# Scaling the input on VectorE instead of GpSimd, with four constants and one DMA rule of the build-time order changed

## The chip, the cores and the metric

The kernel runs on one core of one Trainium2 chip. The metric is the device time of one execution in microseconds; for the kernel before, three timed runs gave 2083.99, 2084.95 and 2100.44 us, with a median of 2084.95 us. In profile rows PE is TensorE (PEld its weight loads), DVE is VectorE, ACT is ScalarE, POOL is GpSimd and SP is SyncE, which issues most DMAs.

## The reference: what is computed

One decoder layer is applied to 256 prompt tokens and to 8 x 8 sample tokens with the same weights. All arrays are float32.

```python
def decoder_layer(x, st, p):
    hn = rmsnorm(x, p['norm1'])                 # x * rsqrt(mean(x^2) + 1e-6) * g
    proj = hn @ p['w_in']                       # 2048 -> 12752 columns
    ...
    y_s5 = s5_mixer(...)                        # diagonal state space
    y_rw = rwkv7_mixer(...)                     # 64-wide matrix state per head
    y_gd = gdn_mixer(...)                       # gated delta rule in chunks of 64,
                                                # with a triangular solve per chunk
    merged = (sigmoid(gt_s5) * (y_s5 @ p['w_br_s5']) + sigmoid(gt_rw) * (y_rw @ p['w_br_rwkv'])
              + sigmoid(gt_gd) * (y_gd @ p['w_br_gdn']))
    x = x + merged @ p['w_out']
    up = rmsnorm(x, p['norm2']) @ p['ffn_w_up']
    ...                                         # depthwise convolution, bias, gate
    return x + (silu(gate) * val) @ p['ffn_w_down'], new_states
```

A final rmsnorm follows. Outputs are the activations of all 320 tokens and the new states.

## The kernel before, in words

**Layout.** Channels lie on the 128 partitions and the 320 tokens on the free axis. Every large product multiplies a 128x128 block of weights by a [128, 320] slice of activations. To keep float32 accuracy with the fast float32r format, both sides are split into a high and a low part (`split`, line 399: ScalarE copies the high part, VectorE subtracts it to get the low part), and `products` (line 573) issues three matmuls per block: high-high, high-low and low-high. These are the wide products; there are 12720 of them, 24 to a step, and a step is one 512 KB weight tile of eight blocks.

**Weights.** `run_steps` (line 568) goes through 530 steps in a fixed order: the S5 input columns, the other columns of `w_in`, the branch products, `w_out`, `w_up` and `w_down`. `load_to` (line 426) fetches a tile into one of four `wraw` buffers with a DMA on SP; the load of step n + 4 is issued when the split of step n is done. ScalarE writes `whi` and VectorE `wlo` in halves of 128x512, into one of three pairs of buffers, so a tile can be split at the earliest when the step three before it has been multiplied.

**Between the wide products.** The recurrent branches are Python generators (`Task`), which are advanced between the blocks of the wide stream by `poll` (line 550). What they issue on TensorE are small products, many of them with tiles of fewer than 128 rows or columns.

**What sets the order.** The order of all instructions on all engines is fixed while the program is built. `Clock` (lines 112 to 225) keeps an estimated time per engine; `issue` (line 182) adds the estimated cost of each instruction, and a DMA's estimated landing time (lines 184 to 201) tells when a task that waits for it may go on. `able` (line 540) decides whether a task may be advanced now: what it reads must be ready, the engines that its next piece uses must not be estimated further than `LEAD` ahead of TensorE, and a piece with small products needs enough `heat`, a credit that wide products build up (lines 218 to 222; `PACE` and `HEAT` on line 115) and small products spend. `BURST` (line 333) is how much estimated time one call of `poll` may add to TensorE, `START` (line 334) the least credit with which a switch from wide to small products may begin, and the 0.0 at the end of line 544 the loss that is assumed of a piece that has not been issued before.

**Places that the change touches.** `norm1` (lines 630 to 661) computes the first rmsnorm. While the S5 columns and the next four columns are multiplied with an input that is not yet normalised (`xg`, made by `prep`, line 625), it gathers the squares, gets `rstd` and then, for each of the 16 channel tiles k, lets GpSimd multiply `x[:, k]` by `rstd` in place (line 658) and, one tile behind, calls `scaled` (line 403): ScalarE writes `high` with the gain `g1` as its scale, VectorE writes `low` as x times gain minus high. From step 16 plus 8 on, the wide products read `high` and `low`; `in_step` (line 678) waits for `norm1` there.

`tri_inverse` (line 1166) inverts the unit triangular matrices of the gated delta rule, 80 of them: four stores write them to the DRAM tile `gdn`, a load brings them back as `triw` with one matrix on each of 80 partitions (rows of 4096 bytes), VectorE eliminates in 60 small tensor_tensor instructions (two for each m from 1 to 30, lines 1190 to 1196), and two more stores and six loads bring the result back. It is used a second time for the rwkv branch.

Of the kernel before, what the change touches and what calls it, by code (L numbers as in the profile page):

```python
# [13 lines left out]
OP = mybir.AluOpType  # L14
# [97 lines left out]
class Clock:  # L112


    PACE, HEAT = 1.15, 800
    LAT = {"pe": 197, "dve": 127, "act": 143, "pool": 120, "dma": 1100}
    TO_SMALL, TO_WIDE, FORM = 90, 160, 140

# [63 lines left out]
    def issue(self, eng, name, outs, ins, a, k):  # L182
        t = self.begin(eng, outs, ins)
        if name == "dma_start":
            n = int(np.prod(outs[0].shape)) * 4
            row = min(run(outs[0]), run(ins[0])) * 4
            cost = n / 360.0 * (1 if row >= 512 else 3)
            if eng == "pool":
                self.t[eng] = t + 1040
                self.later.append((t + 1850, cost))  # L190
                end = max(self.dma, t + 1850) + cost
            else:
                q = self.queue = self.t[eng] = max(self.queue, t + 25) + 450
                while self.later and self.later[0][0] < q + 650:
                    at, c = self.later.pop(0)
                    self.dma = max(self.dma, at) + c
                end = self.dma = max(self.dma, q + 650) + cost
            if row < 4096:
                end += 300 if row >= 2560 else 900
            self.done("dma", outs, ins, end)  # L200
            return t, end + self.LAT["dma"]
        cost = COST[eng](name, outs, ins, a, k)
        if eng == "pe":
            wide = ins[0].dtype == F32R
            form = None if wide else (name, ins[0].shape[0], free_size(ins[0]), outs[0].shape[0])
            if form != self.form:
                t = max(t, self.t[eng] + (self.TO_WIDE if wide else self.FORM if self.form else self.TO_SMALL))
            self.form = form
            lo, n = self.box(outs[0])[1][0] % 128, outs[0].shape[0]
            cols = set(range(lo // 32, (lo + n + 31) // 32))  # L210
            if name == "matmul" and not wide and t == self.t["pe"] and self.cols and not cols & self.cols:
                cost = 0.85 * n
                self.cols |= cols
            else:
                self.cols = cols if name == "matmul" and not wide else None
        end = t + cost
        if eng == "pe":
            used = free_size(outs[0]) * (1 if wide else 4) * ins[0].shape[0] / 128
            if name == "matmul":
                used *= free_size(ins[0]) / 128  # L220
            self.lost = max(self.lost - used + self.PACE * (end - t), 0.0)
            self.heat = min(self.HEAT, self.heat + used - self.PACE * (end - self.t[eng]))
        self.t[eng] = end
        self.done(eng, outs, ins, end)
        return t, self.after("", eng, end)


def run(ap):

    n = 1  # L230
    for s, c in reversed(ap.ap[ap.space != "DRAM":]):
        if s != n and c > 1:
            break
        n *= c
    return n


def free_size(ap):
    return int(np.prod(ap.shape[1:]))
# [90 lines left out]
class Kernel:  # L330
    LEAD = 2100
    SLACK = -300
    BURST = 1500
    START = 600
    IDLE = 300
    PARTS = 2
    MARGIN = 1
# [202 lines left out]
    def able(self, t):  # L540
        now = self.now()
        if t.over or t.busy or t.ready > now + self.SLACK or t.need and len(self.spare) <= t.need or t.cond and not t.cond():
            return False
        uses, lost = self.uses.get(t.place(), (("pe", "dve", "act"), 0.0))
        c = self.clock
        if "pe" in uses and c.heat < (lost if c.form else max(lost, self.START)) and now == c.t["pe"]:
            return False
        return all(e == "pe" or self.clock.t[e] <= now + self.LEAD * (1 if t.rank else 2) for e in uses)

    def poll(self):  # L550

        end = self.clock.t["pe"] + self.BURST
        c = self.clock.t
# [76 lines left out]
    def norm1(self):  # L630

        nc, x = self.nc, self.x
        sums = self.mid.tile([128, 3, 2, T], F32, tag="hh", name="squares")
        acc, *sqs = (sums[:, j] for j in range(3))
        for i in range(KD // 2):
            pair = x[:, 2 * i:2 * i + 2]
            self.wait(pair)
            yield
            sq = sqs[i % 2] if i else acc
            nc.scalar.activation(sq, pair, AF.Square)  # L640
            yield
            if i:
                nc.vector.tensor_tensor(acc, acc, sq, op=OP.add)
        nc.vector.tensor_tensor(acc[:, 0], acc[:, 0], acc[:, 1], op=OP.add)
        yield 1
        p = self.bank()
        nc.tensor.matmul(p, self.mean, acc[:, 0], start=True, stop=True)
        yield
        r = self.st.tile([128, T], F32, tag="gt0", name="rstd")
        self.rstd_of(p, r, acc[:, 1])  # L650
        self.free(p)
        self.rs1 = r
        yield
        yield lambda: self.prepared >= KD // 2
        self.hn = self.halves()
        for k in range(KD + 1):
            if k < KD:
                nc.gpsimd.tensor_tensor(x[:, k], x[:, k], r, op=OP.mult)
            if k:
                self.scaled(x[:, k - 1], self.V("g1", k - 1), *self.hn[k - 1])  # L660
            yield 0

    def first_step(self, i):
# [1568 lines left out]
```

## Time and profile before

| | |
|---|---|
| timed runs | 2083.99, 2084.95, 2100.44 us |
| the profiled execution's own time | 2083.18 us |
| its span, first to last instruction | 2081.3 us |
| mean granted TensorE clock | 0.997 |
| PE busy, matmuls | 2049.8 us, 14557 |
| DVE busy | 1355.7 us |
| ACT busy | 1009.6 us |
| POOL busy | 249.1 us |
| 1000 to 1050 us: matmuls in 50 us | 343 |

The profile lists for each engine when an instruction began, how long it took, and, in square brackets, how long the engine had idled before it and which engine's or DMA's work ended that idle time. All rows name line 298, because a helper records every instruction; the tiles' names tell them apart. A matmul's duration includes its passage through the array, so two matmuls overlap in the rows; what counts is how many begin in a stretch. The time that lies outside the span is 2083.18 - 2081.3 = 1.9 us.

### The profile page before, as it was taken

Reading aid. Unit: us, or ns where it says so; the run is one execution under the profiler, and the core shown is the slowest. Engines: PE = TensorE matmul, PEld = TensorE weight load, DVE = VectorE, ACT = ScalarE, POOL = GpSimd, SP = SyncE. Lnnn points to the kernel's source line nnn. Section 1 sums busy time; section 2 is a strip of 40 time slices with the busy share of each in tenths; the row PEclk is TensorE's granted clock in tenths of the full one; section 3 lists DMA queues with packets and bytes.
Section 4 is the critical chain, followed back from the end, with each engine's and each line's share of the span. In section 5 each row is a group of like instructions: output and inputs, shape, how many; then the busy total and the mean of one; then the engine's idle time right before and its main releaser. Section 6 shows DMA issues by size and latency. Waiting matters only on the chain.

```text
span 2081.3 us, 37242 instructions
## 1 busy us (share of the span) xinstructions
PE 2049.8 (98%) x14557; PEld 1997.6 (96%) x14557; DVE 1355.7 (65%) x2535; ACT 1009.6 (49%) x1911; POOL 249.1 (12%) x467
## 2 busy tenths in 40 slices
PE   8999999999999999999999999999999999999997
PEld 8899999999899999889999999999999999999997
DVE  7989999776267676166855666666544466666444
ACT  6666666643245854343444444444333344444442
POOL 1312102100000000000000222222100022222000
PEclk9999999999999999999999999999999999999999
DMA  7575565556447546357755544544444444444552
GB/s 241 196 245 152 165 194 179 185 173 193 153 166 259 185 153 181 102 179 218 221 178 165 153 151 153 151 147 150 152 152 149 147 151 152 152 146 150 167 153 101
DMA packets 132353, 351.71 MB, mean 169 GB/s; under 512 B 27040, under 2 KB 53712, under 8 KB 131920
## 3 DMA queue, kind: packets, MB, share of 16 engines
q1 hardware_dynamic: 131280, 346.21, 53.0%
q0 software_dynamic: 752, 3.10, 0.4%
q8 instruction: 114, 1.87, 0.4%
q14 instruction: 63, 0.52, 0.1%
q10 hardware_dynamic: 144, 0.01, 0.0%
HBM read 320.20 MB, written 29.06 MB: 168 GB/s over the span
## 4 chain that ended last, share of the span: by engine, by line
PE 58%; DVE 0%; ACT 0%; DVEq 0%; issue 0%; ACTq 0%
PE bank L298 58%; DVE xf L298 0%; DVE acc L298 0%; ACT rstd L298 0%; DVE rstd L298 0%; DVE x L298 0%; ACT sq L298 0%; DVEq L2228 0%; ACTq L298 0%
## 5 line engine op out<-in xcount | busy, mean ns | idle before, releaser
L298 ACT ACTIVATE whi<-wraw 128x512 fp32r<-128x512 f32 x1060 | 614.7, 625 | 672.1 <-issue 376.5
L298 DVE TENSOR_TENSOR wlo<-wraw,whi 128x512 fp32r<-128x512 f32 x1060 | 699.7, 695 | 358.8 <-ACT whi L298 349.7
L298 PE MATMUL bank<-high,whi 128*128 128x320 f32 x1728 | 546.5, 316 | 0.0
L298 PE MATMUL bank<-high,wlo 128*128 128x320 f32 x1728 | 532.6, 308 | 3.4 <-DVE wlo L298 3.4
L298 PE MATMUL bank<-low,whi 128*128 128x320 f32 x1728 | 532.4, 308 | 0.0
L298 PE MATMUL bank<-x2h,whi 128*128 128x320 f32 x1408 | 435.3, 309 | 0.0
L298 PE MATMUL bank<-x2l,whi 128*128 128x320 f32 x1408 | 435.1, 309 | 0.0
L298 PE MATMUL bank<-x2h,wlo 128*128 128x320 f32 x1408 | 435.1, 309 | 0.0
L298 PEld LDWEIGHTS bank<-high,whi 128*128 128x128 f32 x1728 | 324.6, 188 | 14.3 <-issue 9.7
L298 PEld LDWEIGHTS bank<-high,wlo 128*128 128x128 f32 x1728 | 324.5, 188 | 3.9 <-DVE wlo L298 3.9
L298 PEld LDWEIGHTS bank<-low,whi 128*128 128x128 f32 x1728 | 324.9, 188 | 2.0
L298 PEld LDWEIGHTS bank<-x2l,whi 128*128 128x128 f32 x1408 | 264.3, 188 | 0.1
L298 PEld LDWEIGHTS bank<-x2h,whi 128*128 128x128 f32 x1408 | 264.3, 188 | 0.1
L298 PEld LDWEIGHTS bank<-x2h,wlo 128*128 128x128 f32 x1408 | 264.3, 188 | 0.0
L298 PE MATMUL bank<-hidl,whi 128*128 128x320 f32 x704 | 216.5, 308 | 0.0
L298 PE MATMUL bank<-hidh,wlo 128*128 128x320 f32 x704 | 216.5, 307 | 0.0
L298 PE MATMUL bank<-hidh,whi 128*128 128x320 f32 x704 | 216.5, 307 | 0.0
L298 POOL COPY blk<-blk 128x62 f32<-128x62 f32 x88 | 63.7, 724 | 627.6 <-DVE blk L298 627.6
L298 PEld LDWEIGHTS bank<-hidh,whi 128*128 128x128 f32 x704 | 131.9, 187 | 0.0
L298 PEld LDWEIGHTS bank<-hidh,wlo 128*128 128x128 f32 x704 | 131.9, 187 | 0.0
L298 PEld LDWEIGHTS bank<-hidl,whi 128*128 128x128 f32 x704 | 131.9, 187 | 0.0
L298 DVE TENSOR_TENSOR blk<-bank,rstd 128x320 f32<-128x320 f32 x88 | 43.3, 492 | 127.5 <-PE bank L298 127.5
(337 smaller groups left out, 2168.1 us busy)
## 6 DMA issues: line engine op xcount, KB each, us to landing
wraw<-w_in SPq DMA_DIRECT2D x192, 512.0 KB, 3.8
wraw<-w_up SPq DMA_DIRECT2D x176, 512.0 KB, 3.5
wraw<-w_down SPq DMA_DIRECT2D x80, 512.0 KB, 3.5
wraw<-w_out SPq DMA_DIRECT2D x32, 512.0 KB, 3.5
shs<-gst SPq DMA_DIRECT2D x16, 512.0 KB, 3.8
wraw<-w_br_g SPq DMA_DIRECT2D x16, 512.0 KB, 4.6
gates<-ev SPq DMA_DIRECT2D x48, 160.0 KB, 2.4
gt<-gates SPq DMA_DIRECT2D x48, 160.0 KB, 3.6
```

Source lines behind the costliest of these rows:

```text
L298: return f(*a, **k)
```

## The change

```diff
@@ -112,7 +112,7 @@ class Clock:
-    PACE, HEAT = 1.15, 800
+    PACE, HEAT = 1.2, 1000
@@ -197,6 +197,8 @@ def issue, for a dma_start
                 end = self.dma = max(self.dma, q + 650) + cost
             if row < 4096:
                 end += 300 if row >= 2560 else 900
+            elif outs[0].shape[0] < 128:
+                end += 1500
             self.done("dma", outs, ins, end)
@@ -330,8 +332,8 @@ class Kernel:
-    BURST = 1500
-    START = 600
+    BURST = 2000
+    START = 800
@@ -541,7 +543,7 @@ def able
-        uses, lost = self.uses.get(t.place(), (("pe", "dve", "act"), 0.0))
+        uses, lost = self.uses.get(t.place(), (("pe", "dve", "act"), 600))
@@ -655,9 +657,9 @@ def norm1
         for k in range(KD + 1):
             if k < KD:
-                nc.gpsimd.tensor_tensor(x[:, k], x[:, k], r, op=OP.mult)
+                nc.vector.scalar_tensor_tensor(out=x[:, k], in0=x[:, k], scalar=self.V("g1", k), in1=r, op0=OP.mult, op1=OP.mult)
             if k:
-                self.scaled(x[:, k - 1], self.V("g1", k - 1), *self.hn[k - 1])
+                self.split(x[:, k - 1], *self.hn[k - 1])
             yield 0
```

The first rmsnorm's multiplication by `rstd` moves from GpSimd to VectorE and takes the gain with it; `high` becomes a plain copy and `low` a plain subtraction. In the estimate, a DMA whose rows have 4096 bytes or more and whose destination has fewer than 128 partitions (or whose DRAM destination's first axis is shorter than 128) lands 1.5 us later; in this program these are the loads of `triw` and the two stores that follow its elimination. The credit is built up more slowly and to a higher limit, a switch to small products needs more of it, and one call of `poll` may add more. Nothing that is computed changes. Since every estimate feeds the order, instructions move on every engine from the first multiplication on; the wide products stay in the same order among themselves.

On VectorE, just after `rstd` is known and four `ev` tiles are evacuated, the kernel before has these rows (`low` is the low half of the normalised input, `x_sb` the input, `vec` the gains, `wlo` the low half of a weight tile):

```order
L298 TENSOR_TENSOR ev_541<-bank3_66,rstd_510 128x320
L298 SCALAR_TENSOR_TENSOR low_554<-x_sb_95,vec_96,high_553 128x320
L298 SCALAR_TENSOR_TENSOR low_555<-x_sb_95,vec_96,high_553 128x320
L298 TENSOR_TENSOR wlo_551<-wraw_438,whi_550 128x512
L298 SCALAR_TENSOR_TENSOR low_556<-x_sb_95,vec_96,high_553 128x320
L298 SCALAR_TENSOR_TENSOR low_557<-x_sb_95,vec_96,high_553 128x320
```

and the changed kernel these:

```order
L300 TENSOR_TENSOR ev_541<-bank3_66,rstd_510 128x320
L300 SCALAR_TENSOR_TENSOR x_sb_95<-x_sb_95,vec_96,rstd_510 128x320 x2
L300 TENSOR_TENSOR low_554<-x_sb_95,high_553 128x320
L300 TENSOR_TENSOR wlo_551<-wraw_438,whi_550 128x512
L300 SCALAR_TENSOR_TENSOR x_sb_95<-x_sb_95,vec_96,rstd_510 128x320
L300 TENSOR_TENSOR low_555<-x_sb_95,high_553 128x320
```

Each channel tile was one VectorE instruction and is now two. Between two halves of `wlo` there stood the work of two or three tiles, and there stands now that of one or two: six halves stood among the 16 tiles, and 12 stand among them now.

On VectorE, at the start of the elimination in the gated delta branch (`triw`; `kq` is the last work before it, and the numbers of `wlo` grow from step to step), the kernel before has

```order
L298 TENSOR_TENSOR kq_945<-kq_945,af2_4967 128x2x320
L298 TENSOR_TENSOR wlo_5329<-wraw_5243,whi_5328 128x512 x2
L298 TENSOR_TENSOR wlo_5373<-wraw_5282,whi_5372 128x512 x2
L298 TENSOR_TENSOR wlo_5405<-wraw_5320,whi_5404 128x512 x2
L298 MEMSET triw_5353 80x32
L298 TENSOR_TENSOR triw_5353<-triw_5353 80x30 x2
L298 TENSOR_TENSOR triw_5353<-triw_5353 80x2x29 x2
L298 TENSOR_TENSOR triw_5353<-triw_5353 80x3x28 x2
L298 TENSOR_TENSOR triw_5353<-triw_5353 80x4x27 x2
L298 TENSOR_TENSOR triw_5353<-triw_5353 80x5x26 x2
L298 TENSOR_TENSOR triw_5353<-triw_5353 80x6x25 x2
L298 TENSOR_TENSOR wlo_5441<-wraw_5341,whi_5440 128x512
```

and the changed kernel

```order
L300 TENSOR_TENSOR wlo_5441<-wraw_5351,whi_5440 128x512 x2
L300 TENSOR_TENSOR wlo_5474<-wraw_5386,whi_5473 128x512 x2
L300 MEMSET triw_5398 80x32
L300 TENSOR_TENSOR triw_5398<-triw_5398 80x30 x2
L300 TENSOR_TENSOR triw_5398<-triw_5398 80x2x29 x2
L300 TENSOR_TENSOR triw_5398<-triw_5398 80x3x28 x2
L300 TENSOR_TENSOR triw_5398<-triw_5398 80x4x27 x2
L300 TENSOR_TENSOR triw_5398<-triw_5398 80x5x26 x2
L300 TENSOR_TENSOR triw_5398<-triw_5398 80x6x25 x2
L300 TENSOR_TENSOR triw_5398<-triw_5398 80x7x24 x2
L300 TENSOR_TENSOR triw_5398<-triw_5398 80x8x23 x2
L300 TENSOR_TENSOR wlo_5522<-wraw_5414,whi_5521 128x512
```

Counted from the first `wlo`, `wlo_5405` belongs to step 117 and `wlo_5474` to step 119, so step 118 was the first that had to wait for the elimination, and step 120 is it now. The last small product before the elimination stands behind 2658 wide products before and behind 2691 now. From there to the first product that needs the delayed `wlo`, TensorE has 118 x 24 - 2658 = 174 wide products before and 120 x 24 - 2691 = 189 now. Twelve `triw` instructions stood ahead of the next half of `wlo`, and 16 stand there now. On SP, the four stores into `gdn` stood behind the weight load of step 118, which waits for the split of step 114, and stand now behind that of step 119, which waits for the split of step 115; from the last `kq` product's evacuation on, VectorE has three `kq` instructions and four halves of `wlo` up to that point before, and two and three now.

On TensorE, in the rwkv branch's chain of 64-row chunks (`chain`, `uv`, `gm` and `a_r` are its tiles; rows that read `high`, `low` or `yg` are wide products), the kernel before has

```order
L298 MATMUL bank3_66<-chain2_9310,a_r_7767 64x128 x4
L298 MATMUL bank3_66<-uv_8472,gm_8474 64x64 x4
L298 MATMUL bank7_70<-high_553,whi_9283 128x320
L298 MATMUL bank7_70<-low_558,whi_9283 128x320
L298 MATMUL bank7_70<-high_553,wlo_9284 128x320
L298 MATMUL bank3_66<-uv_8472,gm_8474 64x64 x4
```

and the changed kernel

```order
L300 MATMUL bank7_70<-chain2_9481,a_r_7912 64x128 x4
L300 MATMUL bank7_70<-uv_8620,gm_8622 64x64 x8
L300 MATMUL bank6_69<-yg_7546,whi_9385 128x320 x2
L300 MATMUL bank6_69<-yg_7546,wlo_9386 128x320
L300 MATMUL bank3_66<-yg_7546,whi_9453 128x320 x2
L300 MATMUL bank3_66<-yg_7546,wlo_9454 128x320
```

A group of eight that was cut in two by wide products stands in one piece. Over the whole of TensorE, 992 small products stand in 158 bursts between wide products before and in 142 now; of these, 93 and 84 begin or end with a tile of fewer than 128 rows or columns. Inside the bursts the tile size changes 36 times in both.

## The prediction on record

> **What bounds the kernel now.** I read the page first, then the granted clock and the matmuls begun in chosen windows, then what TensorE waited for, and last the timelines around the two longest waits.
>
> ```profile
> span 2081.3 us, 37242 instructions
> PE 2049.8 (98%) x14557; PEld 1997.6 (96%) x14557; DVE 1355.7 (65%) x2535; ACT 1009.6 (49%) x1911; POOL 249.1 (12%) x467
> ```
>
> TensorE is busy for 98% of the span, so only two things can move the time: TensorE standing still, and time that it spends on something other than the 12720 wide products, whose number is the same on both sides.
>
> ```profile
> core 0: us, PE busy (x) PEld busy (x) DVE busy (x) ACT busy (x) POOL busy (x), PEclk, DMA share, GB/s
> 53.00:65.00 12.00, 7.31 (x45) 6.28 (x44) 12.00 (x15) 7.87 (x15) 9.79 (x13) 1.00 0.30 95
> 462.80:470.60 7.80, 4.40 (x20) 4.14 (x19) 7.25 (x23) 1.47 (x3) 0.00 (x0) 0.78 0.17 20
> 850.00:900.00 50.00, 49.74 (x633) 42.73 (x633) 13.31 (x23) 17.87 (x37) 0.56 (x1) 1.00 0.29 93
> 1000.00:1050.00 50.00, 50.00 (x343) 50.00 (x342) 41.11 (x83) 25.35 (x51) 0.00 (x0) 1.00 0.66 206
> ```
>
> The last row is the undisturbed pace: 343 products in 50 us, 0.1458 us each. At that pace 12 us hold 82 products; from 53 to 65 us there are 45, so 37 are missing, 5.4 us. From 462.8 to 470.6 us there are 20 of 53, so 33 are missing, 4.8 us, and here the clock is 0.78: a stretch of 7.8 x 0.22 / 0.5 = 3.4 us ran at half clock.
>
> ```profile
> PEld bank L298 <- DVE wlo L298: 9.8, 7, 3.7
> PEld bank L298 <- DVE tp L298: 2.3, 3, 1.4
> ```
>
> Two of TensorE's waits at its weight loads, each row with the sum, the number and the longest. Those for `wlo` are mostly the two places above. Those for `tp`, 2.3 us in three, are the kind that stands elsewhere: small ones, so that I put what is left to win or lose there at 4 us.
>
> **First part: the input scaling.** These rows show how TensorE and VectorE stand when the scaling begins, and what VectorE's instructions cost while GpSimd multiplies, and at other times (before 44.5 us).
>
> ```profile
> 47.49 2.11 DVE L298 SCALAR_TENSOR_TENSOR low<-x_sb,vec,high 128x320 fp32r<-128x320 f32 x2
> 54.39 0.42 PE L298 MATMUL bank<-xg,wlo 128*128 128x320 f32 x1 [0.80 <-DVE wlo L298]
> ```
>
> ```profile
> L298 DVE SCALAR_TENSOR_TENSOR low<-x_sb,vec,high 128x320 fp32r<-128x320 f32 x16 | 13.4, 881 | 0.0
> L298 DVE TENSOR_TENSOR wlo<-wraw,whi 128x512 fp32r<-128x512 f32 x6 | 6.8, 1130 | 0.0
> L298 POOL TENSOR_TENSOR x_sb<-x_sb,rstd 128x320 f32<-128x320 f32 x16 | 17.0, 1098 | 30.3 <-issue 30.3
> ```
>
> ```profile
> L298 DVE TENSOR_TENSOR wlo<-wraw,whi 128x512 fp32r<-128x512 f32 x24 | 15.7, 687 | 4.3 <-ACT whi L298 4.3
> L298 DVE SCALAR_TENSOR_TENSOR xg<-x_sb,vec,xg 128x320 fp32r<-128x320 f32 x16 | 8.1, 547 | 7.0 <-ACT xg L298 6.8
> L298 DVE TENSOR_TENSOR rstd<-rstd,squares 128x320 f32<-128x320 f32 x1 | 0.5, 493 | 0.0
> ```
>
> ```profile
> 62.21 1.47 DVE L298 SCALAR_TENSOR_TENSOR low<-x_sb,vec,high 128x320 fp32r<-128x320 f32 x3
> ```
>
> While GpSimd's 16 multiplications run, the same `wlo` takes VectorE 1.13 us instead of 0.69, and a `low` 0.88 instead of the 0.55 of the equal `xg` instruction; at 62.21, when GpSimd has just finished, three `low` take 1.47 together. So GpSimd slows VectorE down, and VectorE is late with `wlo`.
>
> The change removes the 16 GpSimd instructions and adds 16 to VectorE, with three operands like `xg`: 8.1 us by that row. The 16 `low` become plain subtractions, 16 x 0.49 = 7.8 us, and the 12 halves of `wlo` that now stand among them cost 12 x 15.7 / 24 = 7.9 us: 23.8 us from 47.5 us on. TensorE uses a half of `wlo` for 12 products, 1.75 us. It stood for the second half from 53.29 on (54.39 less the gap that the row shows, counted between starts), so it needs the first half at 51.5 and the twelfth at 51.5 + 11 x 1.75 = 70.8, that is 23.3 us after 47.5. VectorE is 0.5 us late at the end and nowhere earlier by more. The loss can be 0 at best. The other bound comes from the row of `xg`: there VectorE waited 6.8 us for ScalarE's half of the same 16 tiles, and `low` now waits in the same way for a `high` that ScalarE can only begin when VectorE has scaled the tile. All of it on top would make 7.3 us lost, 1.9 more than now. But the 12 halves of `wlo`, 7.9 us of work that does not read `high`, stand among the tiles and can fill these gaps, so I take 0.5: of 5.4 us, **4.9 us are won**; for the range I let half of the 6.8 us stay unfilled, which leaves 1.5 us, and the upper bound is 5.4. GpSimd has nothing queued behind its 16 multiplications that TensorE soon needs.
>
> **Second part: the short load.** VectorE, SP and TensorE around the elimination:
>
> ```profile
> 446.26 0.69 DVE L298 TENSOR_TENSOR wlo<-wraw,whi 128x512 fp32r<-128x512 f32 x1
> 446.86 0.82 DVE L298 TENSOR_TENSOR kq<-kq,af 128x640 f32<-128x640 f32 x1
> ...
> 462.46 0.18 DVE L298 TENSOR_TENSOR triw<-triw 80x30 f32<-80x30 f32 x1 [8.29 <-DMA triw<-gdn]
> 462.67 3.18 DVE L298 TENSOR_TENSOR triw<-triw 80x30 f32<-80x30 f32 x11
> 465.78 0.68 DVE L298 TENSOR_TENSOR wlo<-wraw,whi 128x512 fp32r<-128x512 f32 x1
> 466.38 1.45 DVE L298 TENSOR_TENSOR triw<-triw 80x168 f32<-80x168 f32 x4
> ```
>
> ```profile
> 450.22 4.55 SPq L298 DMA_DIRECT2D gdn<-nt  x4
> ...
> 456.94 0.34 SPq L298 DMA_DIRECT2D triw<-gdn  x1
> ```
>
> ```profile
> 462.80 0.31 PE L298 MATMUL bank<-low,whi 128*128 128x320 f32 x1
> 466.51 0.41 PE L298 MATMUL bank<-high,wlo 128*128 128x320 f32 x1 [3.40 <-DVE wlo L298]
> ```
>
> VectorE stands 8.29 us behind the load, with the split of step 118 queued behind it and behind 12 eliminations. TensorE uses up what was split and waits from 462.95 (462.80 and one product) to 466.51, 3.6 us, and then runs 3.4 us at half clock. The change does not make the load faster; it changes what stands ahead of it. TensorE has 189 instead of 174 products from the last small product on: 15 x 0.1458 = 2.2 us more. The stores go out one `wlo` half and one `kq` earlier, 0.69 + 0.82 = 1.5 us, and the load, which follows them, with them. Against that, 16 eliminations instead of 12 precede the next `wlo`: the four of the row at 466.38, 1.45 us. The wait becomes 3.6 - 2.2 - 1.5 + 1.45 = 1.35 us. It is 1.35 + 1.5 = 2.85 if the stores are no earlier, and 0 if anything else in front of them shortens.
>
> What a shorter wait does to the clock is bounded by rows: 3.6 us of standing still were followed by half clock, the single waits that make up the 5.4 us from 53 to 65 us were not, with clock 1.00 throughout. So I count the half-clock stretch as gone. The wait of 3.6 and half of the 3.4 make 5.3 us, the missing products 4.8; I take 5.0 for both. Less 1.35 this is **3.6 us won** (2.2 with the wait of 2.85, 5.0 with none).
>
> The Trainium skill, "TensorE: Matmul & The Clock Gate", Part 1, says that half rate follows at least one fully idle window of about 3.4 us; the trace agrees with the length of the half-clock stretch, 3.4 us, and by that rule a wait of 1.35 or 2.85 us leaves the clock alone, which is what the sum has.
>
> **Third part: fewer bursts.** What a burst costs beyond its products:
>
> ```profile
> 555.36 0.31 PE L298 MATMUL bank<-high,wlo 128*128 128x320 f32 x1
> 555.60 0.86 PE L298 MATMUL bank<-vt,nt 64*64 64x128 f32 x6
> 556.40 0.41 PE L298 MATMUL bank<-high,whi 128*128 128x320 f32 x1
> 556.65 0.31 PE L298 MATMUL bank<-low,whi 128*128 128x320 f32 x1
> ...
> 559.35 0.65 PE L298 MATMUL bank<-vt,nt 64*64 64x128 f32 x4
> 559.93 0.42 PE L298 MATMUL bank<-high,whi 128*128 128x320 f32 x1
> ```
>
> ```profile
> 411.60 0.31 PE L298 MATMUL bank<-high,wlo 128*128 128x320 f32 x1
> 411.74 1.03 PE L298 MATMUL bank<-msk,vc 128*128 128x128 f32 x8
> 412.76 0.31 PE L298 MATMUL bank<-low,whi 128*128 128x320 f32 x1
> ```
>
> Six records of 64x64 tiles take 556.40 - 555.60 = 0.80 us to the next wide product and four take 0.58, so one is 0.11. From 555.36 to 556.65 are 1.29 us; two wide products (0.29) and six small (0.66) leave 0.34 us for the two switches. With full tiles, from 411.60 to 412.76, 1.16 us less 0.29 leave 0.87 for eight, 0.11 each: nothing for the switch. So only bursts with small tiles cost, 0.34 us each, and there are 84 instead of 93: 9 x 0.34 = **3.1 us won**. The unknown here is the order inside bursts, where equal tile groups can overlap less; I bound it at 1.5 to 4.5 us.
>
> The other waits of TensorE are shuffled by the new order; I count them at 0, with 4 us either way. The feed-forward part from 1000 us on has no small products but one, and its order is unchanged.
>
> Sum: 4.9 + 3.6 + 3.1 = 11.6 us off the profiled execution's own 2083.2 us (span 2081.3 and 1.9 around it): 2071.6. The median of the runs shown, 2084.95, lies 1.8 above it, so I predict **2073 us**.
>
> **Rivals.** *The wait moves with the load.* If stores and load slip by as much as TensorE gained, the second part is lost: 2073 + 3.6, about 2077 us. For it speaks that VectorE's idle of 8.29 us is far more than the 1.5 us by which the estimate changes; against it stand the 15 more products that the order shows.
>
> *VectorE stays slow.* If GpSimd was not what slowed it, 32 instructions at 0.88 and 12 at 1.13 make 41.8 us against 23.3: TensorE loses 18.5 us between 50 and 90 us instead of 5.4. With the other two gains the sum is 13.1 - 3.6 - 3.1 = 6.4 us more, 2091 us: slower. It decides from a loss of 12.1 us on, where it has eaten the other two gains: that is 35.4 us of VectorE work instead of 41.8, a half of `wlo` at 0.95 us or more. Against it stand the 1.47 us for three `low` at 62.21.
>
> The Trainium skill, "SBUF — State Buffer", on the shared port pair, says that a VectorE instruction with two SBUF inputs and a GpSimd instruction that reads SBUF exclude each other; the trace agrees, 1.13 against 0.69 us, and by that rule this rival falls, since GpSimd has no such work left there.
>
> *Larger bursts drop the clock.* Each half-clock stretch like that at 467 us costs 3.4 / 2 = 1.7 us; five of them make 8.5: 2081.5 us. The row from 850 to 900 us, with 633 mostly small products at clock 1.00, speaks against it.
>
> The Trainium skill, "TensorE: Matmul & The Clock Gate", section "A second HAM failure mode: psum-queue depth-cycling", speaks for it: frequent short idles between groups of matmuls make the clock go to and fro. No run here shows it.
>
> *Everything fits.* If no wait is left at either place, the bursts win their upper bound and the small waits elsewhere vanish, 0.5 + 1.35 + 1.4 + 4 = 7.3 us more are won: 2066 us.
>
> **Chances.** Forecast 0.62, the wait that moves 0.15, slow VectorE 0.07, clock 0.08, everything fits 0.08. The least gains of the three parts are 1.5 + 2.2 + 1.5 = 5.2 us, and 1.2 with the 4 us against: 2084; the rivals but slow VectorE lie between 2066 and 2082. With a microsecond for the spread of the runs the range is 2065 to 2085 us, which leaves out slow VectorE and the outer ends of the others. One per cent, 21 us, is about what a measurement of this kernel can tell from no change: faster by more than that needs a little more than everything fits (0.04), slower three times the price of slow VectorE (0.03), and within 1% is 0.93.
>
> **What would show it.** In the changed profile: no `wlo` above 0.75 us and fewer than 7 products missing from 53 to 65 us; one wait of TensorE below 3 us at the elimination and no clock below 1.00 between 10 and 2060 us; 84 bursts with small tiles. I am wrong if VectorE waits for ScalarE's `high`, if the clock drops elsewhere, or if a wait above 3 us stands at a place that has none now.

## The result, and the profile after

The ratio of the runs is 0.9938, 95% interval 0.9916 to 0.9959; it is a little below the ratio of the medians, 0.9951, because a few executions of the kernel before take some 15 us longer at a lower clock. The forecast was 2073 us, 11.6 us less, in a range from 2065 to 2085.

So the two traces explain 6.2 us, and the other 3.9 lie in what differs between executions of one kernel, of which one each was traced. For the kernel before, the granted clock of the runs shows a part of it: 0.997 at 2083.8 us, 0.995 at 2086.8 us.

The page, and the two stretches of the prediction:

```profile
span 2075.2 us, 37265 instructions
PE 2047.1 (99%) x14557; PEld 1998.3 (96%) x14557; DVE 1354.1 (65%) x2551; ACT 1014.7 (49%) x1916; POOL 231.1 (11%) x451
```

```profile
core 0: us, PE busy (x) PEld busy (x) DVE busy (x) ACT busy (x) POOL busy (x), PEclk, DMA share, GB/s
53.00:65.00 12.00, 12.00 (x84) 12.00 (x83) 12.00 (x26) 7.68 (x16) 0.00 (x0) 1.00 0.52 168
463.00:471.00 8.00, 7.93 (x54) 7.62 (x53) 7.59 (x20) 2.63 (x5) 0.00 (x0) 1.00 0.38 95
700.00:800.00 100.00, 95.92 (x633) 90.76 (x633) 61.25 (x119) 66.09 (x120) 2.08 (x9) 0.97 0.52 161
```

From 53 to 65 us no product is missing now (84 instead of 45, where 82 fit). At the elimination TensorE runs through at full clock. But a new place stands out: from 700 to 800 us TensorE stands still for 4.1 us and the clock is 0.97. The rows there:

```profile
712.98 1.78 PE L300 MATMUL bank<-lora 96*128 96x320 f32 x6
716.20 0.81 PE L300 MATMUL bank<-lora 96*128 96x320 f32 x2 [1.44 <-ACT sa L300]
...
717.04 0.47 PE L300 MATMUL bank<-low,whi 128*128 128x320 f32 x1
...
767.69 0.30 PE L300 MATMUL bank<-high,wlo 128*128 128x320 f32 x1
770.23 0.81 PE L300 MATMUL bank<-tp,mskr 128*128 128x320 f32 x2 [2.23 <-DVE tp L300]
...
771.02 0.31 PE L300 MATMUL bank<-low,whi 128*128 128x320 f32 x1
...
771.65 0.47 PE L300 MATMUL bank<-high,wlo 128*128 128x320 f32 x1
```

```profile
715.62 1.78 ACT L300 ACTIVATE sa<-bank,vec 128x320 f32<-128x320 f32 x4
```

Two small products of the rwkv branch are issued before they can run. The one with `mskr` waits for `tp`, which it reads and VectorE has not finished. The `lora` product does not wait for what it reads: by the kernel's text no operand of it comes from ScalarE. It waits for a `bank`, a tile for TensorE's results, to write into: ScalarE frees banks when it has read them for `sa`, and begins that only at 715.62. TensorE's order is fixed, so all wide products behind the two wait too. After each wait a wide product lasts 0.47 us instead of 0.31: half clock, from 716.92 and from 771.53 us on, 3.41 us each.

In both traces all 12720 wide products are recorded, so one can compare when the same product begins:

| wide product begun | what lies before it | changed less before, us |
|---|---|---|
| 360 | the input scaling | -5.5 |
| 2400 | S5 branch | -4.4 |
| 2880 | the elimination | -10.2 |
| 3600 | the gated delta bursts | -12.2 |
| 4440 | `lora` and `mskr` products | -7.0 |
| 5160 | the end of the rwkv chain | -6.1 |
| 12400 | all else | -6.1 |

12.2 us are won in the first 630 us, a little more than forecast, and 6 are given back up to 950 us.

### The profile page after: what moved, and what is told of

The parts are those of the page before. It is cut to its first block, busy times and chain, and to the rows that moved or that the text cites. A ratio compares the mean times of both kernels' runs of the same rounds, so it can differ in the third digit from the quotient of the medians.

```text
span 2075.2 us, 37265 instructions
## 1 busy us (share of the span) xinstructions
PE 2047.1 (99%) x14557; PEld 1998.3 (96%) x14557; DVE 1354.1 (65%) x2551; ACT 1014.7 (49%) x1916; POOL 231.1 (11%) x451
## 4 chain that ended last, share of the span: by engine, by line
PE 91%; DVE 4%; ACT 2%; issue 1%; DMA 1%; DVEq 0%; ACTq 0%; SPq 0%
PE bank L300 91%; DVE wlo L300 1%; DVE conv L300 1%; ACT whi L300 1%; ACT L300 0%; DVE t L300 0%; ACT tp L300 0%; DMA tp<-rkv 0%; DVE xf L300 0%; DVE triw L300 0%; DVE bu L300 0%; DMA ub<-utn 0%; DVE tp L300 0%; DMA ub<-utf 0%; DMA chain<-wst 0%
```

## The experiments

Unless a diff says otherwise they start from the kernel before; "the constants" are PACE, HEAT, BURST, START and the assumed loss. The kernel before ran beside each group, with medians of 2085.2 to 2085.5 us. Together with before and changed, the first three and three later ones give every combination of the three edits:

| scaling on VectorE | DMA rule | constants | us, median |
|---|---|---|---|
| - | - | - | 2085.66 |
| x | - | - | 2077.23 |
| - | x | - | 2082.78 |
| - | - | x | 2083.44 |
| x | x | - | 2074.29 |
| x | - | x | 2078.38 |
| - | x | x | 2078.80 |
| x | x | x | 2075.54 |

**The scaling alone.**

```diff
-                nc.gpsimd.tensor_tensor(x[:, k], x[:, k], r, op=OP.mult)
+                nc.vector.scalar_tensor_tensor(out=x[:, k], in0=x[:, k], scalar=self.V("g1", k), in1=r, op0=OP.mult, op1=OP.mult)
...
-                self.scaled(x[:, k - 1], self.V("g1", k - 1), *self.hn[k - 1])
+                self.split(x[:, k - 1], *self.hn[k - 1])
```

> The kernel before with the scaling on VectorE alone. My theory: no wait for wlo from 53 to 65 us (5.4 us won); at the elimination TensorE has 190 products of cover as in the changed kernel, but 20 eliminations stand ahead of the next wlo instead of 16, so that a wait of about 1.6 us remains and no half clock (3.4 won); bursts stay 159, nothing won. About 9 us less than before, 2076 us. Rival (the scaling gives only its own stall): 5 us less, 2080 us, with a wait above 3 us at the elimination.

2077.23 us, ratio 0.9956 (0.9932 to 0.9980). No wait at 53 to 65 us, and the order up to product 2598 is the changed kernel's. At the elimination, on VectorE and TensorE:

```profile
459.25 0.15 DVE L298 TENSOR_TENSOR triw<-triw 80x30 f32<-80x30 f32 x1 [3.48 <-issue]
...
459.44 6.29 DVE L298 TENSOR_TENSOR triw<-triw 80x30 f32<-80x30 f32 x19
465.65 1.28 DVE L298 TENSOR_TENSOR wlo<-wraw,whi 128x512 fp32r<-128x512 f32 x2
```

```profile
466.39 0.42 PE L298 MATMUL bank<-high,wlo 128*128 128x320 f32 x1 [1.61 <-DVE wlo L298]
```

The 3.48 us of VectorE's idle time, listed under issue, I take for the wait for the load. TensorE's wait is the expected 1.6 us, with no half clock. So the larger part of what the prediction put down to the short load is already there without the DMA rule: the other order of the scaling stretch runs on through the program and puts the elimination at another place among the products.

**The DMA rule alone.**

```diff
             if row < 4096:
                 end += 300 if row >= 2560 else 900
+            elif outs[0].shape[0] < 128:
+                end += 1500
```

> The kernel before with the DMA rule alone; up to the elimination its order is that of before. My theory: the 5.4 us from 53 to 65 us stay; at the elimination TensorE has 199 products of cover instead of 175 (3.5 us) and 16 eliminations ahead of the next wlo instead of 12 (1.45 us): the wait falls from 3.6 to about 1.5 us and the half clock goes, 3.8 us won, 2081 us. Rival (the wait moves with the load): wait and half clock stay, 2085 us.

2082.78 us, ratio 0.9982 (0.9970 to 0.9995). The wait at the elimination is short and there is no half clock; the wait does not move with the load.

```profile
462.80 0.15 DVE L300 TENSOR_TENSOR triw<-triw 80x30 f32<-80x30 f32 x1 [3.73 <-issue]
...
467.59 0.68 DVE L300 TENSOR_TENSOR wlo<-wraw,whi 128x512 fp32r<-128x512 f32 x1
```

```profile
468.32 0.41 PE L300 MATMUL bank<-high,wlo 128*128 128x320 f32 x1 [0.72 <-DVE wlo L300]
```

VectorE begins the elimination 25.5 us after the last small product, hardly earlier than before (25.9), but two more halves of `wlo` stand ahead of it, so that TensorE's cover lasts longer and its wait is 0.7 us. The time is a miss by 1.8 us against the expected 2081: behind the elimination, at product 2880, the kernel is 2.9 us ahead of before, and at product 3600 only 1.2.

**The constants alone** (the diff's lines on PACE, HEAT, BURST, START and the loss).

> The kernel before with the four constants alone; the order differs from product 2565 on. My theory of the prediction: fewer bursts, about 3 us won; at the elimination 187 products of cover but 20 eliminations ahead of wlo, a wait of 3.5 to 5 us with half clock, 0 to 1 us lost: 2082 to 2083 us. Rival (larger bursts start small products before what they read is ready, as at 714 and 768 us in the changed kernel): 7 us are lost there, 2088 us or more.

2083.44 us, ratio 0.9985 (0.9971 to 0.9998), near the first forecast, but not by its terms. (Two of the 12 executions took 5147 and 6954 us, which nothing here explains; the median of the other ten is 2082.8.) The wait at the elimination is 1.6 us and not 3.5 to 5; but new waits of 0.6, 1.4 and 0.5 us for `wlo` stand ahead of it, from 440 to 451 us, and what holds TensorE back there shortens the wait behind. In the profiled execution two windows of half clock, 6.83 us, follow the waits at 54 to 61 us, which had none in the trace of before.

**The changed order, scaling on GpSimd.** Every instruction keeps the changed kernel's place; only the engine of the 16 scalings and the operands of `high` and `low` are as before (the estimate is told the changed kernel's costs).

```diff
-                nc.vector.scalar_tensor_tensor(out=x[:, k], in0=x[:, k], scalar=self.V("g1", k), in1=r, op0=OP.mult, op1=OP.mult)
+                count("dve", "scalar_tensor_tensor", x[:, k], x[:, k], self.V("g1", k), r)
+                nc.gpsimd.engine.tensor_tensor(x[:, k], x[:, k], r, op=OP.mult)
```

> The changed kernel, every instruction in its order, but the 16 scalings run on GpSimd as before (low has three operands again). It splits the 5.4 us at 53 to 65 us into order and contention. Theory of both: low takes 0.88 and wlo 1.13 us while GpSimd runs, a pair 2.0 us against the 1.75 us in which TensorE uses a half: 1 to 2.5 us of waits, 2077 us. Rival order alone (12 halves of wlo among the tiles instead of 6): no wait, 2075.5 us. Rival GpSimd alone: the full 5.4 us, 2081 us.

2078.02 us, 2.5 above the changed kernel, with two waits for `wlo` in that stretch, 1.6 and 0.5 us. So in this order GpSimd costs some 2 of the 5.4 us, and the rest is the order: 12 halves of `wlo` among the 16 tiles where there had been 6. The other way round, the old order without GpSimd, was not run. By groups on VectorE from 47.5 to 66 us:

```profile
L300 DVE TENSOR_TENSOR wlo<-wraw,whi 128x512 fp32r<-128x512 f32 x8 | 9.5, 1192 | 0.0
L671 DVE SCALAR_TENSOR_TENSOR low<-x_sb,vec,high 128x320 fp32r<-128x320 f32 x10 | 9.5, 964 | 0.0
```

**A busy GpSimd.** The changed kernel with useless work on GpSimd; every instruction of the other engines keeps its place.

```diff
             if k < KD:
                 nc.vector.scalar_tensor_tensor(out=x[:, k], in0=x[:, k], scalar=self.V("g1", k), in1=r, op0=OP.mult, op1=OP.mult)
+                for _ in range(3):
+                    nc.gpsimd.engine.tensor_tensor(self.dummy, self.dummy, r[:, 0:120], op=OP.mult)
```

> The changed kernel, every instruction in its order, with 48 useless multiplications of 128x120 by rstd on GpSimd into a scratch tile, some 20 us from 45 us on; nobody waits for them. Theory of contention: while they run the scaling takes VectorE 0.88 instead of 0.55 us, low 0.8 instead of 0.50, wlo 1.13 instead of 0.70; in some 22 us VectorE does 13.5 us of its work, is 8 us late, and TensorE waits 7 to 9 us: 2083 us. Rival (GpSimd was only in the way because low waited for its results): no change, 2075.5 us.

2083.35 us, 7.8 above the changed kernel. First the changed kernel's groups on VectorE (44 to 72 us), then this one's (44 to 75 us) and GpSimd's:

```profile
L300 DVE TENSOR_TENSOR wlo<-wraw,whi 128x512 fp32r<-128x512 f32 x15 | 10.3, 696 | 0.0
L300 DVE SCALAR_TENSOR_TENSOR x_sb<-x_sb,vec,rstd 128x320 f32<-128x320 f32 x16 | 8.8, 554 | 0.0
L300 DVE TENSOR_TENSOR low<-x_sb,high 128x320 fp32r<-128x320 f32 x16 | 7.9, 497 | 0.1
```

```profile
L300 DVE SCALAR_TENSOR_TENSOR x_sb<-x_sb,vec,rstd 128x320 f32<-128x320 f32 x15 | 10.8, 723 | 0.0
L300 DVE TENSOR_TENSOR low<-x_sb,high 128x320 fp32r<-128x320 f32 x13 | 9.5, 728 | 0.0
L300 DVE TENSOR_TENSOR wlo<-wraw,whi 128x512 fp32r<-128x512 f32 x10 | 9.3, 928 | 0.0
```

```profile
L664 POOL TENSOR_TENSOR dummy<-dummy,rstd 128x120 f32<-128x120 f32 x48 | 28.9, 601 | 34.7 <-DVE rstd L300 31.0
```

Nobody waits for GpSimd here, and no order differs; still each VectorE instruction takes 0.17 to 0.23 us longer. This is contention, shown by itself. The slowdown is weaker than expected (0.73 instead of 0.8 for `low`, 0.93 instead of 1.13 for `wlo`), but GpSimd's work lasted 29 us instead of 20. The Trainium skill, "SBUF — State Buffer", section "Who interferes with whom", says that a VectorE instruction with two SBUF inputs contends with a GpSimd instruction that reads SBUF; this run agrees, 0.73 against 0.50 us.

**The changed kernel with one edit taken back.** First the scaling, then the DMA rule, then the constants (the diffs above, reversed).

> The changed kernel with the scaling back on GpSimd, as before. My theory (scaling won 5.4 us at 53 to 65 us, and as much again by the cover at the elimination): 5.4 us of waits for wlo there; at the elimination 187 products of cover and 16 eliminations ahead of wlo instead of the 20 of the run with the constants alone, so 1.70 - 1.45 = 0.3 us of wait. Time 2082 us, 6 to 7 above the changed kernel. Rival (the three parts help each other): more than 9 us above it.

2078.80 us: a miss, only 3.3 above the changed kernel. The waits at 53 to 61 us are there (5.2 us), and at product 3600 the kernel is 7.5 us behind the changed one, about as expected; at product 5160 it is 1.8 behind. Its `lora` products do not wait, none of its `mskr` products waits more than 0.9 us, and no half clock follows. So what the changed kernel gives back between 3600 and 5160 hangs on where these products happen to fall.

> The changed kernel without the DMA rule; its order differs only from the elimination on. My theory: 20 instead of 16 eliminations stand ahead of the next wlo, 4 x 0.36 us: TensorE waits 1.7 instead of 0.2 us, as in the run with the scaling alone (1.77); what follows is shuffled. 2077 us, 1.5 above the changed kernel. Rival (the rule is what took the wait away): 4 us of wait and half clock, 2080 us or more.

2078.38 us, 2.8 above. The wait at the elimination is 1.37 us, behind 20 eliminations:

```profile
466.74 0.42 PE L298 MATMUL bank<-high,wlo 128*128 128x320 f32 x1 [1.37 <-DVE wlo L298]
```

This is about the 1.5 us expected on top of the changed kernel's 0.2; the rest is elsewhere. In the profiled execution (2090.9 us; one more of the 12 took 2091.3, the others 2074 to 2082) the clock was at half for 30.7 us from 840.0 us on, after a wait of 2.8 us for a load of `x` at 837 us. The last section returns to this.

> The changed kernel with the four constants as before; 159 bursts as before, and the order of the changed kernel up to product 2598. Theory of the prediction (fewer bursts win 3 us): 3 us above the changed kernel, 2078.5 us. My theory now (what the bursts win is paid back at small products that are started before their operands are ready, 714 and 768 us): no difference, 2075.5 us within 1.5. Rival (the constants cost): 2072 us.

2074.29 us, ratio 0.9950 (0.9938 to 0.9962): 1.2 less than the changed kernel. The constants bring nothing on top of the other two edits. Up to product 3000 this kernel is 8.8 us ahead of before and the changed one 9.8, at 3600 it is 8.8 and the changed one 12.2; at 5160 it is 7.9 and the changed one 6.1. The larger bursts do win, and it is lost again.

**BURST alone with the first two edits, and the constants without it.**

> Scaling, DMA rule and BURST = 2000 alone, the other three constants as before: 143 bursts, and lora and tp products at the same places as in the changed kernel. My theory (BURST is the constant that moves the bursts, and what follows from it is paid back): as the changed kernel, 2075.5 us, with 2 us won between products 3000 and 3600 and the waits at lora and tp. Rival (START, PACE, HEAT and the assumed loss cost): 2072.5 us.

> The changed kernel with BURST = 1500 as before and the other constants as changed: 158 bursts. My theory: nothing won between products 3000 and 3600 against the run with none of the constants, and lora and tp stand elsewhere: 2074.3 us within 2. Rival (START, PACE, HEAT and the assumed loss win something of their own): 2072 us or less.

2075.01 and 2074.85 us, the changed kernel's time within a microsecond, as the first theory of each has it. With BURST there are 143 bursts, and `lora` and `mskr` wait 1.3 to 1.7 us at the places of the changed kernel, with no half clock behind them; but of the 2 us expected between products 3000 and 3600 only 0.7 are won (32 bursts with small tiles there, the changed kernel has 29), so BURST does not move the bursts alone. Without it there are 158 bursts, nothing is won there, and other small waits appear.

**The small products later.** The changed kernel with three edits in the rwkv branch: its `lora` products are held back until step 174, and two estimates ahead of the `mskr` products are made longer.

```diff
-        yield
+        yield lambda: self.at >= 174
         yield from self.par(*[factors(i) for i in range(4)])
...
                 tt(e1, cs, s, op=OP.subtract)
+                self.clock.end += 2000
                 yield 1
...
                 stt(out=sq, in0=rk[:, 0], scalar=self.V("rk", i), in1=rk[:, 1], op0=OP.mult, op1=OP.mult)
+                self.clock.end += 2500
                 yield 1
```

> The changed kernel with its estimates in the rwkv branch alone made longer, so that the lora products start a few steps later (product 4179 instead of 4083) and the two products with mskr of each lane 2 to 2.5 us later by the estimate; the order up to product 4083 is the changed kernel's. My theory (the waits at 714 and 768 us, and the half clock that follows them, pay back what the larger bursts won): 1.6 us at lora, 3 us at tp and 1.7 to 3.4 us of half clock go, 2068.5 to 2071 us. Rival (the waits only move to other small products): 2074 us or more.

2068.58 us (2068.0 to 2070.5), ratio 0.9892 (0.9855 to 0.9929): as forecast, 7 us below the changed kernel, and the fastest here. From 700 to 800 us nothing is left, and TensorE's longest waits are these (the first is the first product's, as in every kernel here):

```profile
700.00:800.00 100.00, 100.00 (x690) 96.20 (x688) 63.20 (x115) 62.47 (x121) 2.88 (x9) 1.00 0.54 170
```

```profile
PE bank L300 <- ACT whi L300: 5.6, 1, 5.6
PE bank L300 <- DVE stacked L300: 1.4, 2, 0.7
PE bank L300 <- ACT uparts L300: 0.8, 1, 0.8
```

690 products and no half clock, where the changed kernel had 633 at 0.97. From 640 to 960 us TensorE's waits fall from 5.8 to 0.7 us in sum, and two half-clock stretches of 1.7 us go: 8.5 of the 8.7 us by which the two traces differ, so the waits did not move elsewhere. This shows that the early products cost what the constants had won, and more.

**The same without the constants.** `lora` and `mskr` products stand at the same places between the wide products as in the run above.

> The kernel of the run with the later lora and mskr products, with the four constants as before: 159 bursts instead of 142, lora and mskr products at the same places between the wide products. So the bursts are compared without the waits that paid them back. Theory of the prediction (0.34 us for a burst with small tiles): 95 instead of 84 of them, 3.7 us more, 2072.3 us; what I read from products 3000 to 3600 of the changed kernel, 2.4 us: 2071 us. Rival (the constants win nothing at all): 2068.6 us.

2081.18 us, but this median is of no use: six of the 12 runs took 2071.6 to 2075.1 us and six 2087.3 to 2089.6. The profiled execution is one of the long ones, with half clock for 34.1 us from 851.1 us on:

```profile
850.00:900.00 50.00, 50.00 (x525) 43.13 (x525) 10.71 (x20) 14.44 (x32) 1.47 (x5) 0.66 0.35 103
```

Up to product 4560, ahead of that stretch, the two traces can be compared: with the constants TensorE is 14.1 us ahead of before, without them 11.2; of these 2.9 us, 0.7 were there at product 2400, ahead of the bursts. So the larger bursts are worth 2.2 us there, for 29 instead of 36 bursts with small tiles between products 3000 and 3600: 7 x 0.34 = 2.4 us, as the prediction priced them. The rival that they win nothing falls. The short six, with a mean of 2073.4 us, lie 4.8 above the other kernel; what lies beyond the 2.9 us of the traces is not explained. They lie only 0.9 below the run without the constants and with these products in their old places (2074.29): holding the products back pays chiefly where the constants had moved them.

## The prediction, point by point

**The bound** held: in the stretches compared, what was won or lost was TensorE standing still, its clock, or a change of tiles; VectorE's 16 instructions more cost nothing.

**The input scaling** was forecast to win 4.9 us of 5.4 and won 5.5. VectorE's instructions took 0.55, 0.50 and 0.70 us, as the rows of before said, and it did not come late: the 0.5 us that I kept was not needed, and `low` did not wait for `high`. The reason given was only partly right. That GpSimd slows VectorE is shown by the run with useless work; but in the changed order GpSimd's scaling costs 2.1 us and not 5.4, so by that run the denser halves of `wlo`, which the sum counted only as work to be done, won the other 3.

**The short load** was forecast to win 3.6 us and to leave a wait of 1.35; 5.2 were won (products 2760 to 2880), the wait is 0.2, and the half clock is gone. Of the three terms the 15 products of cover (2.2 us) and the four eliminations (1.45) were right: 20 instead of 16 eliminations cost 1.2 to 1.4 us more in two runs. The term that was too small is the 1.5 us by which stores and load go out earlier:

```profile
449.36 3.26 SPq L300 DMA_DIRECT2D gdn<-nt  x4
...
454.66 0.33 SPq L300 DMA_DIRECT2D triw<-gdn  x1
```

```profile
459.44 0.15 DVE L300 TENSOR_TENSOR triw<-triw 80x30 f32<-80x30 f32 x1 [3.28 <-issue]
...
464.21 0.68 DVE L300 TENSOR_TENSOR wlo<-wraw,whi 128x512 fp32r<-128x512 f32 x1
```

From the last small product to the first elimination it took 25.9 us before and 22.8 us now, 3.1 less and not 1.5: the four stores are issued in 3.26 us instead of 4.55, and from the load's issue to the elimination it takes 4.8 us instead of 5.5. I had said that the load becomes no faster. And the name was wrong: cover and earlier stores came with the scaling's order (1.6 us of wait with it alone); the DMA rule took the eliminations ahead of `wlo` from 20 to 16, 1.2 us.

**The bursts** were forecast to win 3.1 us. 84 bursts with small tiles are there as counted (the trace of before, counted by the first and last record of each burst, has 95 and not 93), and the price was about right, 2.2 us for seven of them where it could be measured without other differences. But the net gain of the constants is nothing (2075.5 with, 2074.3 without).

**The other waits**, counted at 0 with 4 us either way, are the step that failed. From product 3600 on the changed kernel pays 1.6 us at `lora`, about 3 at the `mskr` products, and 1.7 for each of two stretches of half clock, 8 us, where the kernel before had some 2 us of waits: 6.1 us net. That the measured median still lies only 2.5 us from the forecast is luck, for two reasons: the first two parts won 2.2 us more than forecast, and the profiled execution of the changed kernel is slower than its median, that of before faster, so that the medians differ by 10.1 us where the traces differ by 6.2.

**The rivals.** The wait did not move with the load. VectorE did not stay slow. Half clock did come, twice, and the sentence that no clock below 1.00 would stand between 10 and 2060 us was wrong; but it came after waits of TensorE, not from larger bursts, and went when the waits were taken away. By its own sign ("if the clock drops elsewhere") the prediction was wrong there. It had held single waits as long as those from 53 to 65 us, 2.6 us at most, to be harmless from one trace of them; a wait of 2.4 us, at 768 us, was followed by half clock.

## What to carry to other kernels

Where one engine's order is fixed and it is the bound, an early small operation costs its whole wait, and every operation behind it pays: look for each place where the bound engine waits, and move that operation later by its estimate, before tuning how much goes into a burst (7 us here, against 2). An edit that changes an order early shuffles everything behind it, so count its effect stage by stage at equal work, and test constants in pairs whose orders agree at the places that matter. A GpSimd instruction that nobody waits for is not free where VectorE is close to late.

## What the runs showed of the hardware

**Half clock after short waits.** In all 14 traces every change of the clock within the program lies on a grid of 3.41 us, which begins with the first clock record, at 8.7 to 11.8 us. So the stretches at half clock last 3.41 us or multiples (6.83, 30.72, 34.13), apart from the last one, which the program's end cuts off. What tells the windows apart is, with two exceptions, how long TensorE stands still within one of them. Between the first record and 2050 us six windows at full clock have 1.94 to 2.81 us without a matmul, and half clock follows each of them: 2.78 before, 2.11 at 768 us in the changed kernel, 1.94 and 2.05 in the two runs with GpSimd's work, 2.05 with the constants alone, 2.81 without the DMA rule. No other has more than 1.86, and only two of those are followed by half clock: one with 1.44 us, at 714 us in the changed kernel among `lora` products of 96 rows, and one with 0.66 us ahead of a long stretch (below). The wait of 2.5 us at 56 us, the same in four traces, was followed by half clock in one: there 2.05 us of it fell into one window, in the other three 1.86 at most. (No run moved a wait against the grid, so that this is read from the traces and not tested.) The Trainium skill, "TensorE: Matmul & The Clock Gate", Part 1, gives the 3.4 us as the length of a window that must be idle; the length agrees, but here a window idle for 1.94 of 3.41 us was enough each time, and the measurement decides.

**A long stretch.** In two traces, of the run without the DMA rule and of the later products without the constants, the clock stayed at half for 31 to 34 us, from 840 and 851 us on, while TensorE had matmuls all the time, most of them with 32x32 and 64x64 tiles, 15 to 17 us lost. Both began within 3 us of the end of a wait for a load of the tile `x` (2.8 and 1.1 us). With the later products and the constants the same stretch ran at 1.00:

```profile
850.00:900.00 50.00, 50.00 (x691) 43.12 (x689) 16.23 (x31) 19.13 (x39) 1.46 (x5) 1.00 0.47 155
```

What decides between long and short executions of one and the same program, six of 12 each with the later products and without the constants, stays open: no run took that wait alone away.
